# A hybrid decoder step on one core: weight splitting, softmax scaling and small copies are moved between VectorE, GpSimd and ScalarE, and a small inverse is spread over more steps

## The chip, the cores and the metric

The kernel runs on one core of a Trainium2 chip. The metric is device microseconds of the whole program, the median of several runs. TensorE multiplies matrices, VectorE (DVE in the profile), ScalarE (ACT) and GpSimd (POOL) work on elements, SyncE (SP) issues most transfers. Each engine executes its own instructions in order and waits on semaphores for the others.

## The reference

One layer of a decoder with a half-step SwiGLU FFN at either end and two groups of heads side by side in the middle. 256 prompt tokens and 8 decode tokens go through the same weights, 264 columns in all. The model width is 2048, the FFN width 5504, everything is float32.

```python
x = x + 0.5 * swiglu(rmsnorm(x, n1), f1g, f1u, f1d)
h = rmsnorm(x, nm)
proj = h @ w_in                                   # 38 tiles of 128 columns
o_att, k_buf, v_buf = attend(q, k, v, sinks)      # 16 query heads, 4 key/value heads, window 128
o_rwkv, shift, S = rwkv_time_mix(proj[..., ATT_COLS:], shift0, wkv0, ...)   # 16 heads of 64
x = x + concatenate([o_att, o_rwkv], -1) @ w_out
x = x + 0.5 * swiglu(rmsnorm(x, n2), f2g, f2u, f2d)
y = rmsnorm(x, final_norm)
```

Attention adds a relative bias, takes the maximum with a learned sink, and divides by the sum of the exponentials and the sink's own. In the RWKV part

```python
a = sigmoid(a0 + al @ a2); kk = k * k_k; k = k * (1 + (a - 1) * k_a)
S = S * exp(logw) + (S @ -kk) outer (kk * a) + v outer k;  y = S @ r      # for each token
```

## The kernel before, in words

**Layout.** Activations are kept transposed: a tile has 128 features on the partitions and the 264 tokens as columns. A weight tile of 128x128 is the stationary operand, an activation tile the moving one.

**Weights.** `chunk` loads up to four weight tiles (128x512 float32) with a transfer on SP's queue into a `raw` buffer (six of them). ScalarE rounds it to a `hi` part (line 123). A `tensor_tensor` subtraction on the engine that `chunk` is given computes the remainder `lo` (line 58 is the helper for all such operations); before the change it is VectorE in every case. There are four `hi` and four `lo` buffers. `gemm` then multiplies each weight tile three times (hi by hi, hi by lo, lo by hi) into an `acc` bank. A chunk's operations are emitted at high priority.

**Stages.** First FFN, then the mixing stage, then the second FFN. In the mixing stage `win` multiplies the 38 projection tiles one after the other: two for the low-rank parts, 24 for the eight pairs of RWKV heads (receptance, key, value), four for keys and values (`LKV` = 26 is the first of them), eight for queries. Then three passes of the output projection each take some of the 16 `mixed` tiles and add to all 16 output tiles:

```python
PASS = [[0,1,2,3],[8,9,10,11,4,5],[6,7,12,13,14,15]]      # 0-7 RWKV pairs, 8-15 attention tiles
```

Pass 0 thus has one chunk of four weight tiles for each output tile; passes 1 and 2 have a chunk of four and one of two.

**Tasks.** All the small work of the mixing stage is written as generators that are stepped once (`tick`) after every chunk of `win` and of the output projection; this sets the order of the program. `prep` prepares a pair of RWKV heads; `chain` does a batch of two pairs (four batches); `attend` does two prompt heads; `kvtask` writes keys and values; `dec_load` and `dec_attend` do the decode tokens' attention for four query tiles at once. The scheduler then orders the instructions of each engine by priority and by a model of when they become ready, so that the steps of a task are laid between chunks, not exactly where they were written.

**The chain of a batch.** When both `prep` are done, `X` and `Y` (tag `Xt`) are read back from DRAM, rearranged so that a 32x32 triangular block lies in the columns of one partition. After `DWAIT` steps, 30 elimination steps of two VectorE operations each run, with a step of the task after each `NSTEP` of them. `Y` is stored to DRAM (`scr2`, `sb` in the profile) by four transfers and read back by four as `TT`, now with rows on partitions. After `DWAIT` more steps VectorE adds the unit diagonal to the four blocks of `TT` and transposes two of them into `TN`. TensorE completes the 64x64 inverse from it. A product gives `W` and the values; VectorE copies the value part into `uv` in four pieces (line 595). State and output follow, three more chunk states are scanned, and `gnorm` normalises (reciprocals at line 677). `X`, `Y` and `TN` have one buffer each, `uv` three, of which the decode caches take two at a time.

**Softmax.** For each head VectorE adds the bias and takes the maximum, ScalarE exponentiates, VectorE forms the reciprocal of the sum and scales both parts (128x256 and 128x128; line 65 is the helper). TensorE transposes the result.

**Decode attention** waits in `dec_load` for a batch to be done (the third for the first call, the last for the second), loads its caches into `uv` buffers, and clears `qb`, which shares two `bk` buffers with `prep` and with the scores of `dec_attend`.

Of the kernel before, what the change touches and what calls it, by code (L numbers as in the profile page):

```python
# [9 lines left out]
AF = mybir.ActivationFunctionType  # L10
ALU = mybir.AluOpType
AX = mybir.AxisListType

P = 128
# [7 lines left out]
NPAIR = 8  # L22
NSH = 26
NIN = 38
HALF = (slice(0, 64), slice(64, 128))
# [4 lines left out]
NS, NO, NY, NH, NT, NLD = 38, 8, 8, 40, 18, 6  # L30
NWARM = 14
NGM, NKR, NUV, NTT, NBT = 10, 5, 3, 2, 5
NSTEP = 4
DWAIT = (8,8,8,4)
PW = (2, 1, 3, 2, 2)
ALPHA = math.exp(-0.5)
LKV = 26
# [5 lines left out]
VMU, VKK, VKA, VA0, VRK, VLW, VLB, VSK, VSD = 64, 90, 98, 106, 114, 122, 130, 138, 154  # L43
# [4 lines left out]
def body(tc, I, O):  # L48
    nc = tc.nc
    V, A, G, TE, SP = nc.vector, nc.scalar, nc.gpsimd, nc.tensor, nc.sync  # L50
    cnt = [0]

    def uid(s):
        cnt[0] += 1
        return f"{s}{cnt[0]}"

    def tt(e, out, a, b, op):
        return e.tensor_tensor(out=out, in0=a, in1=b, op=op)  # L58
# [4 lines left out]
    def ts(e, out, a, s1, op0, s2=None, op1=None):  # L63
        k = {} if op1 is None else dict(op1=op1)
        e.tensor_scalar(out=out, in0=a, scalar1=s1, scalar2=s2, op0=op0, **k)

    def act(out, in_, f, **k):
        return A.activation(out=out, in_=in_, func=f, **k)  # L68

    def bc(ap, shape):  # L70
        return ap.broadcast_to(list(shape))
# [23 lines left out]
    with ExitStack() as ctx:  # L95
# [20 lines left out]
        def chunk(src, n, e, ahead=True):  # L116
            w = n * P
            with tc.high_priority() if ahead else nullcontext():
                raw = wp.tile([P, CH * P], F32, tag="raw", bufs=NRAW, name=uid("raw"))
                hi = wp.tile([P, CH * P], F32R, tag="hi", bufs=NHL, name=uid("hi"))  # L120
                lo = wp.tile([P, CH * P], F32R, tag="lo", bufs=NHL, name=uid("lo"))
                SP.dma_start(raw[:, :w], src)  # L122
                A.copy(hi[:, :w], raw[:, :w])  # L123
                tt(e, lo[:, :w], raw[:, :w], hi[:, :w].bitcast(F32), ALU.subtract)
            return hi, lo

        def gemm(ps, src, xs, step=None, rng=None, ahead=True):
            n = len(xs)
            for k0 in range(0, n, CH):
                k1 = min(n, k0 + CH)  # L130
                if rng and k0 not in rng:
                    continue
                hi, lo = chunk(src[:, k0 * P:k1 * P], k1 - k0, V, ahead)
                for k in range(k0, k1):
                    xh, xl = xs[k]
                    c = slice((k - k0) * P, (k - k0 + 1) * P)
                    mm(ps[:, :T], hi[:, c], xh, k == 0, False)
                    mm(ps[:, :T], hi[:, c], xl, False, False)
                    mm(ps[:, :T], lo[:, c], xh, False, k == n - 1)
                if step:  # L140
                    step()

        vec = cp.tile([P, NVEC], F32, name="vec")
# [13 lines left out]
        def vc(i):  # L157
            return vec[:, i:i + 1]
# [173 lines left out]
        def mixing_body(mx, n2, n3, XD):  # L332
            def fix(shape, name):
                return mx.tile(list(shape), F32, name=name)
# [9 lines left out]
            ident, bo, cm = C[:, CID:CID + P], C[:, CBO:CBO + P], C[:, CCM:CCM + P]  # L344
# [8 lines left out]
                G.memset(pj[:, 0:1], 0.0)  # L353
            nmu = fix((P, NSH), "nmu")
            mu = vec[:, VMU:VMU + NSH]
            ts(V, nmu, mu, -1.0, ALU.mult, 1.0, ALU.add)
            tt(V, ss, ss, bc(mu.unsqueeze(2), (P, NSH, NB)), ALU.mult)
            nbat = len(BATCH)
# [2 lines left out]
            mixed = [None] * 16  # L361
            have = [False]

            def win(t):
                ps = acc()
                gemm(ps, I["win"][t], n2.xs, tick)
                if not have[0]:
                    n2.rstd(rs)
                    have[0] = True
                return ps  # L370
# [20 lines left out]
            def prep(p, bt, k, xrr, xk, xv):  # L391
# [7 lines left out]
                sg, a = tmp(), tmp()  # L399
# [20 lines left out]
                rk = tmp((P, T + 2 * NB))  # L420
                stt(b, b, 1e24, kk, ALU.min, ALU.mult)
                tt(V, b, b, a, ALU.mult)
                ts(V, a, a, 1.0, ALU.subtract, vc(VKA + p), ALU.mult)
                kx = a
                stt(kx, a, 1.0, xk, ALU.add, ALU.mult)
                stt(rk[:, :T], xrr, vc(VRK + p), kx, ALU.mult, ALU.mult)
# [43 lines left out]
                for h in range(2):  # L470
# [3 lines left out]
                    for blk in range(2):  # L474
                        x = blk * 32
# [12 lines left out]
                for c in range(4):  # L488
                    for h in range(2):
                        r, o = HALF[h], HALF[1 - h]  # L490
# [24 lines left out]
            def chain(bt):  # L515
                n = bt.n
                while bt.left:
                    yield
                nr = n * 16
                ng = P // nr  # L520
                if ng == 3:
                    ng = 2
                nj = 32 // ng
                X = ring((ng * nr, 32, 32), "X", 1)
                Y = ring((ng * nr, nj, 32), "Xt", 1)
# [4 lines left out]
                TT = ring((P, n * 4, 64), "TT", NTT)  # L530
                for h in range(2):
                    G.memset(TT[h * 64 + 32:h * 64 + 64, :, 0:32], 0.0)
                yield from pause(DWAIT[bt.i])
                for s in range(1, 31):
                    m, w = -(-s // ng), 31 - s
                    t = ring((ng * nr, m, w), "st", 2)
                    shp = (ng * nr, m, w)
                    tt(V, t, bc(X[:, s:s + 1, s + 1:], shp), bc(Y[:, :m, s:s + 1], shp), ALU.mult)
                    tt(V, Y[:, :m, s + 1:], Y[:, :m, s + 1:], t, ALU.add)
                    if s % NSTEP == 0:  # L540
                        yield
                for g in range(ng):
                    SP.dma_start(scr2[bt.i].rearrange("r (j g t) -> g r j t", g=ng, t=32)[g], Y[g * nr:(g + 1) * nr])
                yield from pause(1)
                for h in range(2):
                    for blk in range(2):
                        x = h * 64 + blk * 32
                        SP.dma_start(TT[x:x + 32, :, blk * 32:blk * 32 + 32],
                                     scr2[bt.i].rearrange("(h b m) (s t) -> h b s m t", h=2, b=2, s=32)[h, blk])
                yield from pause(DWAIT[bt.i])  # L550
                for h in range(2):
                    for blk in range(2):
                        x = h * 64 + blk * 32
                        v = TT[x:x + 32, :, blk * 32:blk * 32 + 32]
                        tt(V, v, v, bc(ident[x:x + 32, x:x + 32].unsqueeze(1), (32, n * 4, 32)), ALU.add)
                TN = ring((P, n * 4, 32), "TN", 1)
                for h in range(2):
                    V.transpose(TN[h * 64:h * 64 + 32], TT[h * 64:h * 64 + 32, :, 0:32])
# [1 line left out]
                ps = mp()  # L560
                for k in range(n):
                    for c in range(4):
                        for h in range(2):
                            j = k * 4 + c
# [7 lines left out]
                ps = mp()  # L572
# [9 lines left out]
                uv = bt.UV  # L582
# [8 lines left out]
                for k in range(n):  # L591
                    v = wus[k].rearrange("p (c t) -> p c t", c=4)
                    A.copy(W[:, k], v[:, 1:4, 0:64])
                    for h in range(2):
                        V.tensor_copy(uv[HALF[h], :, k, HALF[h]], v[HALF[h], :, 64:128])  # L595
                yield
                pbs = [mp() for _ in range(n)]
                for k in range(n):
                    for c in range(1, 4):
                        x = (c - 1) * P  # L600
# [6 lines left out]
                for k in range(n):  # L607
                    v = pbs[k][:, :384].rearrange("p (c t) -> p c t", c=3)
# [3 lines left out]
                for k in range(n):  # L612
                    for c in range(4):
                        x = (k * 4 + c) * 64
# [3 lines left out]
                for k in range(n):  # L618
                    for c in range(4):
                        x = (k * 4 + c) * 64  # L620
# [8 lines left out]
                for c in range(1, 4):  # L629
                    ps = mp()  # L630
# [4 lines left out]
                    for k in range(n):  # L635
                        for h in range(2):
                            r = HALF[h]
                            x = (k * 4 + c) * 64
# [20 lines left out]
                for k in range(n):  # L659
                    p, o = bt.p0 + k, Ys[k]  # L660
# [42 lines left out]
            def softmax(s, mxv, sinks, n):  # L703
                nm, sm, es = (ring((P, 2), "st" + x, 6) for x in "abc")
                ts(V, nm[:, :n], mxv[:, :n], -1.0, ALU.mult)
                for j in range(n):
                    act(s[j], s[j], AF.Exp, bias=nm[:, j:j + 1], accum_out=sm[:, j:j + 1])
                act(es[:, :n], nm[:, :n], AF.Exp, bias=sinks)
                tt(V, sm[:, :n], sm[:, :n], es[:, :n], ALU.add)
                V.reciprocal(sm[:, :n], sm[:, :n])  # L710
                for j in range(n):
                    ts(V, s[j], s[j], sm[:, j:j + 1], ALU.mult)

            def attend(t, q):
                p = t // 4
# [114 lines left out]
            for kind, i in SEQ:  # L830
                if kind == "b":
                    bt = newbatch(i)
                    for k in range(BATCH[i]):
                        p = bt.p0 + k
                        x = [shifted(2 + 3 * p + j, tmp()) for j in range(3)]
# [5 lines left out]
                elif kind == "kv":  # L841
                    w, p = i // 2, i % 2
                    ps = win(LKV + i)
                    x = slot()
# [4 lines left out]
                else:  # L849
                    ps = win(LKV + 4 + i)  # L850
# [5 lines left out]
                    if i % 4 == 3:  # L856
                        p = i // 4
                        d = spawn(dec_attend(p, qs[4 * p:]))
# [18 lines left out]
            k0 = 0  # L877
            for pi, ks in enumerate(PASS):
                now = need(ks)
                drain(now, [g for g in tasks if g not in now])  # L880
                with tc.high_priority():
                    for k in ks:
                        split(k)
                for o in range(KD):
                    ps = acc()
                    gemm(ps, I["wout"][o, :, k0 * P:(k0 + len(ks)) * P], [mixed[k] for k in ks], tick)
                    with tc.high_priority():
                        tt(V, xr[o], ps[:, :T], xr[o], ALU.add)
                    if pi == len(PASS) - 1 and o < CH:
                        n3.split(xr[o], tag="y")  # L890
                for k in ks:
                    mixed[k] = None
                k0 += len(ks)
# [42 lines left out]
        n2, n3 = Norm(VGM), Norm(VG2)  # L936
# [105 lines left out]
```

## Time and profile before

| | |
|---|---|
| median of 3 runs | 2026.01 us (2024.55 to 2027.55) |
| profiled execution, its own time | 2027.84 us |
| its span, first to last instruction | 2026.1 us |
| granted TensorE clock, mean | 0.994 |
| first FFN, about | 0 to 770 us |
| mixing stage, about | 770 to 1260 us |
| second FFN, about | 1260 to 2026 us |

A row of a group gives line, engine, operation, tiles and shapes, the count, then busy time in us and the mean ns of one, then the engine's idle time just before these instructions and what ended most of it. A row of the timeline gives start, duration, engine, line, operation and in brackets the idle time before and its releaser. A row of stretches gives busy time and count for each engine, the granted TensorE clock (PEclk, 1.00 is full), the share of time that the DMA engines were busy, and GB/s. In the chain of waits a row gives start, length and what the time went to.

### The profile page before, as it was taken

To read this page: it belongs to the slowest core of one execution; us is meant where nothing else is said; L and a number is where in the kernel's file an instruction comes from. 1 tells how busy PE (TensorE), PEld (TensorE's weight loads), DVE (VectorE), ACT (ScalarE), POOL (GpSimd) and SP (SyncE) were. 2 spreads that over 40 slices of the span, in tenths; PEclk is the share of its full clock that TensorE was granted. 3 is DMA by queue.
4 is the path that set the end of the run, shared out by engine and by line. 5 is a ranking of instruction groups with operands and counts; after the bars stand their busy time and mean duration, and the time that the engine had idled before them with its cause. 6 is when DMAs were issued, how large, how long until landed. Compare 5 with 4: busy or idle time off the path is not lost.

```text
span 2026.1 us, 45592 instructions
## 1 busy us (share of the span) xinstructions
PE 1994.1 (98%) x17126; PEld 1956.0 (97%) x17126; DVE 1324.4 (65%) x2674; ACT 1041.4 (51%) x2054; POOL 240.8 (12%) x342
## 2 busy tenths in 40 slices
PE   9999999999999999999999899999999999999998
PEld 9999999999999999998888789999999999999998
DVE  5865555655556577678778766775666666566665
ACT  5644444444444466665454555554444444444445
POOL 0401001010110122111110000120101101010012
PEclk9999999999999999999999999999999999999999
DMA  6565565655556566554456335565565555655654
GB/s 228 177 187 196 183 192 189 186 184 177 185 171 191 181 205 205 154 157 124 141 148 174 117 102 188 172 185 176 191 182 194 180 191 190 187 191 180 197 180 144
DMA packets 228798, 358.73 MB, mean 177 GB/s; under 512 B 42568, under 2 KB 83680, under 8 KB 228576
## 3 DMA queue, kind: packets, MB, share of 16 engines
q1 hardware_dynamic: 222112, 347.28, 54.6%
q10 hardware_dynamic: 6464, 8.54, 1.3%
q8 instruction: 134, 2.20, 0.4%
q14 instruction: 88, 0.72, 0.1%
HBM read 347.58 MB, written 10.22 MB: 177 GB/s over the span
## 4 chain that ended last, share of the span: by engine, by line
PE 94%; DVE 2%; DMA 2%; ACT 1%; SPq 1%; issue 1%; ACTq 0%; DVEq 0%
PE acc L74 85%; PE m L74 8%; DVE lo L58 1%; DMA TT<-sb 0%; DMA sb<-Xt 0%; DVE y L58 0%; DMA raw<-in_gu 0%; DMA ld<-in_sT 0%; DVE st L58 0%; SPq L122 0%; DVE Xt L58 0%; ACT t L68 0%; DVE uv L595 0%; DMA Xt<-sa 0%; PE m L495 0%
## 5 line engine op out<-in xcount | busy, mean ns | idle before, releaser
L58 DVE TENSOR_TENSOR lo<-raw,hi 128x512 fp32r<-128x512 f32 (+2 forms) x1304 | 871.8, 673 | 552.5 <-ACT hi L123 526.5
L123 ACT CAST hi<-raw 128x512 fp32r<-128x512 f32 (+2 forms) x1304 | 779.3, 602 | 861.6 <-PE acc L74 776.3
L74 PE MATMUL acc<-s,hi 128*128 128x264 f32 x5940 | 1107.3, 286 | 3.9 <-DVE s L58 1.6
L74 PEld LDWEIGHTS acc<-s,hi 128*128 128x128 f32 x5940 | 922.9, 188 | 10.0 <-ACT hi L123 2.2
L74 PE MATMUL acc<-s,lo 128*128 128x264 f32 x2970 | 848.3, 286 | 4.4 <-DVE lo L58 4.4
L74 PEld LDWEIGHTS acc<-s,lo 128*128 128x128 f32 x2970 | 559.5, 189 | 9.1 <-DVE lo L58 5.6
L74 PE MATMUL acc<-t,hi 128*128 128x264 f32 x2752 | 503.1, 284 | 0.0
L74 PEld LDWEIGHTS acc<-t,hi 128*128 128x128 f32 x2752 | 426.4, 188 | 0.0
L74 PE MATMUL acc<-t,lo 128*128 128x264 f32 x1376 | 389.0, 285 | 0.0
L58 POOL TENSOR_TENSOR t<-t,t 128x264 f32<-128x264 f32 (+1 forms) x148 | 150.7, 1018 | 1150.6 <-ACT hi L123 790.4
L74 PEld LDWEIGHTS acc<-t,lo 128*128 128x128 f32 x1376 | 258.4, 188 | 0.1
L74 PE MATMUL acc<-y,hi 128*128 128x264 f32 x648 | 124.5, 284 | 0.0
L74 PEld LDWEIGHTS acc<-y,hi 128*128 128x128 f32 x648 | 101.3, 188 | 0.2
L74 PE MATMUL acc<-y,lo 128*128 128x264 f32 x324 | 92.2, 285 | 0.0
L58 DVE TENSOR_TENSOR t<-acc,t 128x264 f32<-128x264 f32 x156 | 67.4, 432 | 36.8 <-PE acc L74 36.5
L58 POOL TENSOR_TENSOR o<-o,o 128x264 f32<-128x264 f32 x43 | 36.4, 846 | 222.7 <-ACT o L68 217.8
L74 PE MATMUL acc<-o,hi 128*128 128x264 f32 x324 | 62.8, 284 | 0.0
L74 PEld LDWEIGHTS acc<-y,lo 128*128 128x128 f32 x324 | 60.7, 187 | 0.0
L61 DVE SCALAR_TENSOR_TENSOR s<-acc,s 128x264 f32<-128x264 f32 x96 | 40.5, 427 | 16.0 <-PE acc L74 15.5
L74 PEld LDWEIGHTS acc<-o,hi 128*128 128x128 f32 x324 | 50.0, 188 | 0.0
L74 PE MATMUL m<-s,hi 128*128 128x264 f32 x260 | 48.5, 285 | 0.0
L61 DVE SCALAR_TENSOR_TENSOR x<-acc,x 128x264 f32<-128x264 f32 x96 | 40.5, 426 | 10.1 <-PE acc L74 9.6
(234 smaller groups left out, 1295.9 us busy)
## 6 DMA issues: line engine op xcount, KB each, us to landing
raw<-in_gu SPq DMA_DIRECT2D x688, 256.0 KB, 3.3
raw<-in_dn SPq DMA_DIRECT2D x224, 256.0 KB, 2.7
raw<-in_win SPq DMA_DIRECT2D x152, 256.0 KB, 3.5
raw<-in_dn SPq DMA_DIRECT2D x160, 192.0 KB, 2.7
raw<-in_wout SPq DMA_DIRECT2D x48, 256.0 KB, 3.3
raw<-in_wout SPq DMA_DIRECT2D x32, 128.0 KB, 2.9
xsp<-x ACTq DMA_DIRECT2D x16, 132.0 KB, 3.2
s<-xsp SPq DMA_DIRECT2D x16, 132.0 KB, 4.0
```

What stands on the lines that cost most here:

```text
L58: return e.tensor_tensor(out=out, in0=a, in1=b, op=op)
L61: return V.scalar_tensor_tensor(out=out, in0=a, scalar=s, in1=b, op0=op0, op1=op1)
L74: TE.matmul(out, lhsT, rhs, start=start, stop=stop, **k)
L123: A.copy(hi[:, :w], raw[:, :w])
```

## The change

- `gemm` counts the chunks of the whole program. Where `share` is set (query tiles of `win`, and all output-projection passes), chunks with an odd count have their `lo` computed by GpSimd, the others by VectorE.
- `NSTEP` goes from 4 to 2 and `DWAIT` from (8, 8, 8, 4) to (8, 8, 8, 8).
- The unit diagonal is no longer added to `TT` by VectorE: GpSimd writes ones on the diagonal of `Y` before it is stored, four memsets per batch.
- Of the four value copies of a batch, two go to ScalarE.
- Of the two softmax scalings of a head, the first goes to GpSimd, the second to ScalarE.
- In `prep`, `(a - 1) * k_a` goes from VectorE to ScalarE, as an activation with scale `k_a` and bias `-k_a`; `-k_a` is computed once on GpSimd.

```diff
-NSTEP = 4
-DWAIT = (8,8,8,4)
+NSTEP = 2
+DWAIT = (8, 8, 8, 8)
...
-        def gemm(ps, src, xs, step=None, rng=None, ahead=True):
+        nch = [0]
+
+        def gemm(ps, src, xs, step=None, rng=None, ahead=True, share=False):
...
-                hi, lo = chunk(src[:, k0 * P:k1 * P], k1 - k0, V, ahead)
+                nch[0] += 1
+                hi, lo = chunk(src[:, k0 * P:k1 * P], k1 - k0, G if share and nch[0] % 2 else V, ahead)
...
+            nka = fix((P, NPAIR), "nka")
+            ts(G, nka, vec[:, VKA:VKA + NPAIR], -1.0, ALU.mult)
...
-                gemm(ps, I["win"][t], n2.xs, tick)
+                gemm(ps, I["win"][t], n2.xs, tick, share=t >= LKV + 4)
...
-                ts(V, a, a, 1.0, ALU.subtract, vc(VKA + p), ALU.mult)
+                act(a, a, AF.Identity, scale=vc(VKA + p), bias=nka[:, p:p + 1])
...
+                for g in range(ng):
+                    d = Y[g * nr:(g + 1) * nr].rearrange("p j t -> p (j t)")
+                    G.memset(d[:, g:nj * 32:32 + ng], 1.0)
                 for g in range(ng):
                     SP.dma_start(scr2[bt.i].rearrange("r (j g t) -> g r j t", g=ng, t=32)[g], Y[g * nr:(g + 1) * nr])
...
-                for h in range(2):
-                    for blk in range(2):
-                        x = h * 64 + blk * 32
-                        v = TT[x:x + 32, :, blk * 32:blk * 32 + 32]
-                        tt(V, v, v, bc(ident[x:x + 32, x:x + 32].unsqueeze(1), (32, n * 4, 32)), ALU.add)
...
-                    for h in range(2):
-                        V.tensor_copy(uv[HALF[h], :, k, HALF[h]], v[HALF[h], :, 64:128])
+                    V.tensor_copy(uv[HALF[0], :, k, HALF[0]], v[HALF[0], :, 64:128])
+                    A.copy(uv[HALF[1], :, k, HALF[1]], v[HALF[1], :, 64:128])
...
-                for j in range(n):
-                    ts(V, s[j], s[j], sm[:, j:j + 1], ALU.mult)
+                ts(G, s[0], s[0], sm[:, 0:1], ALU.mult)
+                A.mul(s[1], s[1], sm[:, 1:2])
...
-                    gemm(ps, I["wout"][o, :, k0 * P:(k0 + len(ks)) * P], [mixed[k] for k in ks], tick)
+                    gemm(ps, I["wout"][o, :, k0 * P:(k0 + len(ks)) * P], [mixed[k] for k in ks], tick, share=True)
```

## The prediction

> **What bounds the kernel now.** I read the page first, then stretches of 5 us through the mixing stage (projections, RWKV chain, attention, output projection), the timelines of all engines where TensorE loses time, and the groups by form for prices.
>
> ```profile
> span 2026.1 us, 45592 instructions
> PE 1994.1 (98%) x17126; PEld 1956.0 (97%) x17126; DVE 1324.4 (65%) x2674; ACT 1041.4 (51%) x2054; POOL 240.8 (12%) x342
> 69.34 700.37 PE acc L74 x5760
> ```
>
> TensorE bounds it. The third row is a piece of the chain of waits in the first FFN: 700.37 / 5760 = 0.1216 us for a large matmul, so a full weight chunk (12 of them) is 1.46 us. The FFNs leave nothing to take and the change doesn't touch them. What can move lies in the mixing stage:
>
> ```profile
> core 0: us, PE busy (x) PEld busy (x) DVE busy (x) ACT busy (x) POOL busy (x), PEclk, DMA share, GB/s
> 915.00:920.00 5.00, 3.08 (x74) 3.01 (x76) 4.74 (x13) 0.38 (x2) 0.00 (x0) 0.84 0.33 91
> 965.00:970.00 5.00, 3.04 (x23) 2.62 (x22) 4.78 (x11) 1.17 (x2) 0.19 (x1) 1.00 0.32 74
> 995.00:1000.00 5.00, 3.92 (x89) 3.66 (x86) 4.81 (x14) 2.39 (x6) 0.39 (x2) 0.70 0.38 108
> 1045.00:1050.00 5.00, 2.92 (x22) 2.50 (x22) 4.75 (x11) 1.49 (x3) 1.90 (x6) 1.00 0.43 118
> 1100.00:1105.00 5.00, 3.12 (x19) 2.33 (x17) 5.00 (x20) 3.29 (x10) 1.44 (x2) 1.00 0.93 295
> 1145.00:1150.00 5.00, 4.00 (x56) 3.18 (x56) 3.71 (x18) 3.19 (x12) 0.00 (x0) 1.00 0.61 203
> 1150.00:1155.00 5.00, 2.61 (x26) 1.73 (x27) 3.14 (x9) 4.21 (x13) 0.00 (x0) 1.00 0.06 20
> 1155.00:1160.00 5.00, 3.56 (x11) 2.68 (x12) 4.98 (x15) 0.00 (x0) 1.63 (x7) 0.74 0.08 21
> 1160.00:1165.00 5.00, 3.38 (x15) 1.89 (x14) 2.01 (x10) 3.46 (x10) 1.06 (x7) 0.50 0.44 129
> 1165.00:1170.00 5.00, 4.89 (x20) 3.86 (x21) 3.44 (x11) 4.02 (x15) 2.46 (x4) 0.50 0.00 0
> 1170.00:1175.00 5.00, 5.00 (x34) 4.45 (x35) 4.03 (x19) 2.66 (x9) 0.49 (x1) 0.90 0.03 11
> sum 395.00, PE 375.10 PEld 340.96 DVE 301.84 ACT 221.14 POOL 40.31; mean PE 4.75 PEld 4.32 DVE 3.82 ACT 2.80 POOL 0.51
> ```
>
> The sum row covers 835 to 1230 us: TensorE idles 395.0 - 375.1 = 19.9 us there. That, with the clock that falls after idle stretches, is about all that any change here can win. The largest piece is 1145 to 1175, between the first and second output-projection pass: idle 1.00 + 2.39 + 1.44 + 1.62 + 0.11 = 6.56 us; the clock deficits times the busy time, 0.26 x 3.56 + 0.5 x 3.38 + 0.5 x 4.89 + 0.1 x 5.00, add 5.6. I call these 12.1 us the seam. In the five other stretches shown VectorE is at 4.7 us or more of 5 while TensorE starves: a late VectorE, after a stall of its own or under a backlog.
>
> ```profile
> 898.52 0.41 DVE L58 TENSOR_TENSOR TT<-TT,C 32x256 f32<-32x256 f32 x1 [4.29 <-DMA TT<-sb]
> 915.46 0.85 DVE L595 COPY uv<-m 64x256 f32<-64x256 f32 x2
> 916.83 0.86 DVE L595 COPY uv<-m 64x256 f32<-64x256 f32 x2
> 916.46 0.33 PE L74 MATMUL m<-BT,W 64*64 64x64 f32 x4 [1.89 <-DVE uv L595]
> 1152.21 0.33 PE L805 MATMUL m<-C,bk 128*128 128x128 f32 x1 [3.21 <-DVE bk L65]
> 1153.54 3.46 DVE L677 RECIPROCAL t<-t 128x264 f32<-128x264 f32 x2 [1.19 <-ACT t L68]
> 1161.45 0.37 ACT L744 COPY t<-m 128x256 f32<-128x256 f32 x1 [6.93 <-PE m L742]
> 1165.08 1.42 PE L74 MATMUL acc<-s,hi 128*128 128x264 f32 x3 [1.24 <-ACT s L870]
> ```
>
> First row: VectorE stands 4.29 us at the head of its queue for the readback of the inverse. Next three: TensorE waits until the value copies are done. Last four, the seam: the second pass needs the first decode attention; its softmax scaling (L65 on `bk`) ends late, then group norm of the last RWKV batch (L677) holds VectorE for 3.46 us in the middle, and large matmuls resume at 1165.08.
>
> **The change part by part.** Prices:
>
> ```profile
> L58 DVE TENSOR_TENSOR lo<-raw,hi 128x512 fp32r<-128x512 f32 x1112 | 771.7, 696 | 534.1 <-ACT hi L123 508.2 <-PE acc L74 10.7
> L58 DVE TENSOR_TENSOR TT<-TT,C 32x256 f32<-32x256 f32 x16 | 6.7, 417 | 12.8 <-DMA TT<-sb 12.5
> L595 DVE COPY uv<-m 64x256 f32<-64x256 f32 x16 | 6.7, 421 | 0.3
> L65 DVE TENSOR_SCALAR t<-t,stb 128x256 f32<-128x256 f32 x16 | 6.1, 381 | 0.3
> L65 DVE TENSOR_SCALAR t<-t,stb 128x128 f32<-128x128 f32 x16 | 4.5, 279 | 0.0
> L65 DVE TENSOR_SCALAR t<-t,vec 128x264 f32<-128x264 f32 x8 | 2.8, 350 | 0.0
> L500 ACT COPY BT<-m 64x256 f32<-64x256 f32 x16 | 5.9, 366 | 0.2
> L68 ACT ACTIVATE t<-t,sta 128x128 f32<-128x128 f32 x16 | 6.2, 388 | 0.0
> L58 POOL TENSOR_TENSOR t<-t,t 128x264 f32<-128x264 f32 x74 | 82.5, 1115 | 1105.7 <-ACT hi L123 790.4 <-DVE t L58 293.5 <-ACT t L68 21.8
> L58 POOL TENSOR_TENSOR s<-y,s 128x264 fp32r<-128x264 f32 x4 | 2.9, 744 | 41.3 <-PE m L74 40.0 <-ACT s L870 1.3
> L532 POOL MEMSET TT<- 32x256 f32 x8 | 2.4, 306 | 5.4 <-PE m L74 5.1
> ```
>
> *Chunks to GpSimd.* Counting chunks through the program, the first query chunk and the first chunk of each pass are odd. So GpSimd gets 16 of 32 query chunks, 8 of 16 in pass 0, and in passes 1 and 2 the four-tile chunk of every output tile (32), VectorE the two-tile ones: 56 x 0.696 = 39.0 us leave VectorE. No row shows a 512-wide one on GpSimd. From below: 0.744 us for 264 columns; without any fixed part 512 cost 1.44, with the memset's 0.31 as fixed part 1.15. From above: 1.115 x 512 / 264 = 2.16. I take 1.5, nearest to the undisturbed row with the same output type. TensorE needs 18 x 0.1216 = 2.19 us for an output tile of passes 1 and 2, so GpSimd keeps pace even at 2.16, barely, and four hi/lo pairs give some 5 us of cover. GpSimd and VectorE slow each other:
>
> ```profile
> 1320.93 0.84 DVE L58 TENSOR_TENSOR lo<-raw,hi 128x512 fp32r<-128x512 f32 x1 [0.64 <-ACT hi L123]
> 1326.50 0.69 DVE L58 TENSOR_TENSOR lo<-raw,hi 128x512 fp32r<-128x512 f32 x1 [0.43 <-ACT hi L123]
> ```
>
> The first ran beside a GpSimd operation in the second FFN, the second alone: 0.15 us each, at most 56 x 0.15 = 8 us of VectorE time back, well under 39.0. The Trainium skill (GPSIMD Engine Reference, Engine selection) speaks against this edit: elementwise work belongs on VectorE, two-input operations being about 2x slower on GpSimd. Doubling 0.696 would make an estimated 1.39 us, within the bounds above, still below 2.19; by the rule alone the sum would stay as it is. Whether the trace agrees at this width no row shows.
>
> *Softmax scaling.* 16 x 0.381 + 16 x 0.279 = 10.6 us leave VectorE; 16 on GpSimd at 0.4 to 1.1 us (VectorE's price; the 264-wide two-input row), 16 on ScalarE at 0.388. In a head's own chain this is 0 to 0.7 us longer, covered by other heads. The four decode scalings go the same way, two to each. Both engines now wait for the reciprocal with weight chunks queued behind: `hi` on ScalarE, `lo` on GpSimd, TensorE behind both.
>
> *Value copies.* Per batch two of four go to ScalarE (0.366): 0.84 us less between product and TensorE. Waits like the 1.89 us stand at two batches' tails (915 and 995): 1.7 us, and some clock: **-2**.
>
> *Unit diagonal.* 16 x 0.417 = 6.7 us leave VectorE, one add (0.42) per batch is on the way to TensorE. Added: four GpSimd memsets of the diagonal before the store, 0.1 to 0.31 each and a handover. SP's four stores wait for them, weight loads behind; six raw buffers, 8.8 us, cover that. The 4.29 us wait itself stays: the transpose now stands where the add stood. **0**, bounds -1.7 to +4.
>
> *Key scaling.* 8 x 0.350 leave VectorE; on ScalarE at most 0.388 x 264 / 128 = 0.80 each, with a handover there and back inside a preparation that has other work beside it: **0**, bounds -1 and +2.
>
> *NSTEP and DWAIT.* An inverse takes 15 task steps instead of 7, so all chain tails stand 8 steps later, the last 16 (its two waits go from 4 to 8). At one step per chunk that is 12 and 23 us or more. By the program's count the last chain still ends some 40 steps ahead of pass 2, its consumer. Its stores, readbacks and group norm now queue behind work of attention 0 to 3. The X/Y loads of the next batch, one buffer, fall at the step of this batch's readback; both wait on SP for the same store, weights behind: cover as above. **+1**, bounds -2 to +6.
>
> *The seam.* Ahead of it VectorE loses 24 of those chunks, 16.7 us, and half the prefill scalings, 5.3: 22 us, more than the 12.1 it lasts; group norm's 3.46 us falls later. Decode attention can start earlier, under pass 0. Bounds 0 and -12.1. I take **-7**: TensorE's and ScalarE's legs of it remain.
>
> The stretch at 1100 (VectorE 5.00 of 5, TensorE idle 1.88): **-1**. Late GpSimd halves: **+1.5** (one visible wait), bounds 0 and +20.
>
> Sum: -7 - 2 - 1 + 1 + 1.5 + 0 = -7.5 us. The profiled execution took 2027.84, 1.7 over its span; minus 7.5 gives 2020.3. Against the median of 2026.01, the middle of the runs, 2018.5: I say **2019**.
>
> **Rivals.**
>
> *One: the seam moves.* The first seam closes, but the last batch's chain and the second decode attention, which needs a value buffer of that batch, end after pass 1 has run dry. For it:
>
> ```profile
> 1158.11 0.31 POOL L771 MEMSET bk<- 128x256 f32 x1 [56.38 <-DVE t L61]
> 1215.02 0.56 POOL L823 COPY o<-bk 128x8 f32<-128x8 f32 x4 [44.53 <-ACT bk L821]
> ```
>
> The second decode attention delivers at 1215, just as pass 2 begins: no slack. Against it: 16 more chunks move off VectorE within pass 1. It gives back 5 to 9 of the 10 us won, so -7.5 becomes -2.5 to +1.5: 2023 to 2028. Chance 0.13: 0.09 "same", 0.02 on either side.
>
> *Two, slower: GpSimd stands.* It executes in order. The rows just shown had it waiting 56 and 45 us, free then because nobody needed it. If such a wait, or one of the 18 scalings, stands ahead of a weight half longer than the cover (5.8 us of chunks less 0.62 for `hi` and 1.5 for itself, some 3.7 us), TensorE stops. VectorE's like waits (965 and 1045) cost TensorE 1.96 and 2.08 us each. Six to ten such are 12 to 20 us, less the 9 of the other terms (-7 - 2 - 1 + 1): +3 to +11, and up to +18 where the seam stays too: 2029 to 2044. Against it: the order is laid out by expected readiness, and few GpSimd operations remain between halves. Chance 0.25.
>
> *Three, slower: GpSimd sets the pace.* If a half beside VectorE's own work takes 2.6 us, passes 1 and 2 grow by 32 x 0.41 = 13 us: about 2032. Only a wide form slower than proportional does it. Chance 0.08.
>
> *Four: all VectorE stalls go too*, about 20 us: 2006. Chance 0.06. That the edit isn't what it says I exclude.
>
> **How the numbers follow.** The forecast (2009 to 2021) has 0.48. A measurement tells about 0.2%, 4 us, from no change. Faster: 0.48 + 0.06 + 0.02 of rival one = 0.56; same 0.09; slower 0.25 + 0.08 + 0.02 = 0.35. Both signs hold much, so the forecast's own range stands beside the wide one: 2009 to 2021 against 2006 to 2036, which leaves out some 0.04 below (half of rival four and little else) and 0.13 above (half of rival two).
>
> **What would show it.** Right: VectorE busy near 1324 - 60 us; 56 `lo` on POOL at 1.3 to 1.9 us; no stretch of TensorE under 4 us of 5 between passes 0 and 1, clock 1.00 there; the readback wait of some 4 us now before the transpose. Wrong: TensorE waiting on `lo` of POOL or on a scaling, idle at the start of pass 2, more table loads on ScalarE than 30 (each 1.28 us by this row),
>
> ```profile
> L68 ACT ACT_TABLE_LOAD x30 | 38.5, 1283 | 4.4 <-PE m L74 2.7 <-PEq L1034 1.2
> ```
>
> or the seam as before.

## The result, and the profile after

| | before | after |
|---|---|---|
| median | 2025.57 us (2024.55 to 2027.55, 4 runs) | 2008.21 us (2007.07 to 2011.2, 4 runs) |
| profiled execution, its own time | 2027.84 us | 2008.12 us |
| mean granted TensorE clock | 0.994 | 0.998 |

The ratio is 0.9906, with a 95% interval of 0.9894 to 0.9918: faster by 0.94%, some 17 to 19 us. The forecast was 7.5 us. The sign and the place were right, the size was not: 2008.21 lies just outside the forecast's own range (2009 to 2021) and inside the wide one (2006 to 2036).

From the page of the changed kernel, its span and the busy time of each engine:

```profile
span 2006.0 us, 45669 instructions
PE 1980.9 (99%) x17126; PEld 1947.9 (97%) x17126; DVE 1300.9 (65%) x2550; ACT 1053.8 (53%) x2089; POOL 336.6 (17%) x433
```

The second FFN now begins about 19 us earlier. Stretches of the changed kernel: two at the start of pass 0, then the 30 us in which the seam lay before, then the sum's stretch of the prediction:

```profile
core 0: us, PE busy (x) PEld busy (x) DVE busy (x) ACT busy (x) POOL busy (x), PEclk, DMA share, GB/s
1110.00:1115.00 5.00, 4.37 (x47) 3.33 (x45) 2.96 (x11) 2.40 (x7) 2.24 (x6) 1.00 0.89 251
1115.00:1120.00 5.00, 4.47 (x34) 3.83 (x34) 2.66 (x13) 4.82 (x20) 4.57 (x13) 1.00 1.02 343
1145.00:1175.00 30.00, 30.00 (x275) 26.91 (x274) 20.91 (x58) 18.96 (x51) 12.20 (x12) 1.00 0.32 91
835.00:1230.00 395.00, 381.92 (x4007) 352.45 (x4006) 291.63 (x822) 242.46 (x608) 134.85 (x197) 1.00 0.53 149
```

Where the passes lie now is seen from the first transpose of the first decode attention, which pass 1 needs, and from the first two-tile half, which belongs to the first output tile of pass 1:

```profile
1111.07 0.27 PE L808 MATMUL m<-C,bk 128*128 128x128 f32 x1
1157.63 0.43 DVE L58 TENSOR_TENSOR lo<-raw,hi 128x256 fp32r<-128x256 f32 x1 [0.49 <-ACT hi L123]
```

Before, that transpose came at 1152.21 us, between the two passes. Now the first decode attention is done ahead of pass 0 (VectorE adds the first output tile of pass 0 at 1123 us), and pass 1 follows pass 0 at about 1160 us without a gap. Nothing of the seam's 12.1 us is left. The start of pass 0 idles 0.63 + 0.53 = 1.2 us, at full clock.

Over 835 to 1230 us TensorE idles 395.00 - 381.92 = 13.1 us, 19.9 before. Outside the seam that is 13.1 against 13.3: there the idle time has moved, not shrunk. To follow both losses I cut 770 to 1260 us of every kernel into 5 us stretches and added up the idle time (5 less TensorE's busy time) and the clock's deficit (one less PEclk, times the busy time): before 19.9 + 8.4 = 28.3 us, after 13.1 + 0.0. That is 15.2 of the 19.7 us between the two profiled executions, 12.1 of it the seam; the rest I can't place. (The sum is a guide only: over the kernels below it differs from the change of time by up to 6.5 us.)

In these two executions 8.4 of the 15.2 us are clock. That part varies from one execution to the next: of two variants below, `p_order` idles 22.6 us and lost 1.1 to the clock, `s_uv` 21.1 and 13.3. Over all executions the mean granted clock is 0.994 to 0.995 for the kernel before and 0.998 for the changed one, an estimated 6 to 7 us of 2008.

Where TensorE still waits, from the changed kernel's waits between 835 and 1230 us (engine and line, what it waited for: us in total, times, longest):

```profile
PE m L74 <- ACT t L68: 4.0, 4, 1.6
PE acc L74 <- DVE lo L58: 2.8, 3, 1.4
PE m L448 <- DVE S L61: 1.8, 1, 1.8
PE m L74 <- DVE st L58: 1.5, 2, 1.2
PE m L74 <- ACT uv L598: 1.3, 1, 1.3
```

No matmul waits for a weight half or a scaling of GpSimd (weight loads do once, for 0.2 us); before, `bk` of VectorE alone held it 3.21 us. The moved work, from the groups by form of the changed kernel:

```profile
L58 POOL TENSOR_TENSOR lo<-raw,hi 128x512 fp32r<-128x512 f32 x56 | 73.2, 1309 | 69.5 <-ACT hi L123 45.8 <-PE acc L74 17.3 <-DMA s<-xsp 2.5
L65 POOL TENSOR_SCALAR t<-t,stb 128x256 f32<-128x256 f32 x16 | 15.8, 988 | 18.6 <-DVE stb L713 8.0 <-ACT o L756 3.3 <-DVE st L58 3.2
L549 POOL MEMSET Xt<- 32x8 f32 x16 | 1.7, 105 | 33.1 <-DMA Xt<-sa 21.1 <-DVE st L58 10.9 <-PE acc L74 0.4
L715 ACT ACTIVATE t<-t,stb 128x128 f32<-128x128 f32 x16 | 6.4, 401 | 1.3 <-DVE stb L713 1.3
L68 ACT ACTIVATE t<-t,nka,vec 128x264 f32<-128x264 f32 x8 | 4.9, 608 | 12.0 <-DVE t L58 11.9
L68 ACT ACT_TABLE_LOAD x31 | 39.8, 1283 | 10.4 <-DVE S L61 4.9 <-PE m L74 2.1 <-DVE s L58 1.8
```

Every GpSimd duration lies inside its bounds; on ScalarE the softmax scaling took 0.401 us for the 0.388 taken, the key scaling 0.608, under its bound of 0.80, and there is one table load more. GpSimd does stand at the head of its queue (33.1 us ahead of the diagonal, 18.6 ahead of the scalings), and nobody pays for it in this order.

### The profile page after: what moved, and what is told of

The parts are those of the page before. It is cut to its first block, busy times and chain, and to the rows that moved or that the text cites. A ratio compares the mean times of both kernels' runs of the same rounds, so it can differ in the third digit from the quotient of the medians.

```text
span 2006.0 us, 45669 instructions
## 1 busy us (share of the span) xinstructions
PE 1980.9 (99%) x17126; PEld 1947.9 (97%) x17126; DVE 1300.9 (65%) x2550; ACT 1053.8 (53%) x2089; POOL 336.6 (17%) x433
## 4 chain that ended last, share of the span: by engine, by line
PE 92%; DVE 3%; DMA 2%; ACT 1%; issue 1%; SPq 1%; POOL 0%; DVEq 0%; ACTq 0%; POOLq 0%
PE acc L74 85%; PE m L74 7%; DVE lo L58 1%; DMA sb<-Xt 0%; DVE Xt L58 0%; DVE st L58 0%; DMA TT<-sb 0%; DMA raw<-in_win 0%; DMA raw<-in_gu 0%; ACT L68 0%; ACT hi L123 0%; DVE y L58 0%; SPq L122 0%; ACT t L68 0%; DMA Xt<-sa 0%
## 5 line engine op out<-in xcount | busy, mean ns | idle before, releaser
L58 DVE TENSOR_TENSOR lo<-raw,hi 128x512 fp32r<-128x512 f32 (+1 forms) x1248 | 853.4, 688 | 542.6 <-ACT hi L123 522.5
L58 POOL TENSOR_TENSOR lo<-raw,hi 128x512 fp32r<-128x512 f32 x56 | 73.2, 1309 | 69.5 <-ACT hi L123 45.8
```

## Experiments

Two theories stood at the start. *Relief*: what counts is VectorE time taken off ahead of the seam, so the shared chunks carry most of the gain. *Order*: any of the edits lays the stages out anew, and the gain is that of the order. Undoing one part at a time tells them apart: by relief the chunks must cost the most, by order no part has a price of its own.

**One part undone in the changed kernel.** `u_share` gives all chunks back to VectorE, `u_steps` the old step constants, `u_soft` both softmax scalings to VectorE, `u_small` the value copies, the unit diagonal and the key scaling together.

```diff
 u_share
-                hi, lo = chunk(src[:, k0 * P:k1 * P], k1 - k0, G if share and nch[0] % 2 else V, ahead)
+                hi, lo = chunk(src[:, k0 * P:k1 * P], k1 - k0, V, ahead)
 u_steps
-NSTEP = 2
-DWAIT = (8, 8, 8, 8)
+NSTEP = 4
+DWAIT = (8,8,8,4)
 u_soft
-                ts(G, s[0], s[0], sm[:, 0:1], ALU.mult)
-                A.mul(s[1], s[1], sm[:, 1:2])
+                for j in range(n):
+                    ts(V, s[j], s[j], sm[:, j:j + 1], ALU.mult)
 u_small
-                act(a, a, AF.Identity, scale=vc(VKA + p), bias=nka[:, p:p + 1])
+                ts(V, a, a, 1.0, ALU.subtract, vc(VKA + p), ALU.mult)
 ...
```

> The changed kernel with all weight halves back on VectorE (steps, scaling, diagonal, value copies and key scaling stay changed). Theory A (relief: the 17 us come from VectorE's load ahead of the seam, whose largest part are the 24 chunks, 16.7 us): the seam between passes 0 and 1 comes back in most of its length, 2018 to 2024 us. Theory B (order: they come from the chain tails being emitted 8 to 16 steps later, so that the first decode attention is ready before the last batch's group norm): still 2008 to 2012 us, no seam.

> The changed kernel with NSTEP = 4 and DWAIT = (8, 8, 8, 4) again. Theory A (relief): within 4 us of the changed kernel, 2006 to 2012 us, no seam. Theory B (order): the last batch's tail stands in front of the first decode attention again, the seam is back with a granted clock under 0.9 in it, 2018 to 2026 us.

> The changed kernel with both softmax scalings on VectorE again. Theory A (relief): 10.6 us of VectorE back, half of it ahead of the seam: 2010 to 2015 us. Theory B (order): within 3 us of the changed kernel, 2006 to 2011 us.

> The changed kernel with all four value copies, the unit diagonal and the key scaling on VectorE again. Theory A (relief, with the value copies on TensorE's path at the batches' tails): 2 to 4 us of idle TensorE back at the tails and some granted clock, 2010 to 2014 us. Theory B (order): within 2 us of the changed kernel, 2006 to 2010 us.

| kernel | median us | ratio to before (95%) | lost of the 0.94% |
|---|---|---|---|
| `u_share` | 2014.5 | 0.9936 (0.9921 to 0.9951) | 0.30 |
| `u_steps` | 2012.2 | 0.9930 (0.9915 to 0.9945) | 0.24 |
| `u_soft` | 2011.49 | 0.9928 (0.9911 to 0.9944) | 0.22 |
| `u_small` | 2015.64 | 0.9945 (0.9930 to 0.9960) | 0.39 |

Each loss is known to about 0.19 (the two intervals together). By these figures every part carries 4 to 8 us. Relief by the number of microseconds moved falls: 39.0 us of chunks are worth 0.30%, and some 13 us of small work (copies, adds, key scaling) 0.39%.

**One part alone on the kernel before.** If the parts add up, each alone brings what its undoing cost (additive); if the seam closes only when all are there, each alone brings little (joint).

```diff
 a_share: only the GpSimd chunks;  a_steps: only NSTEP and DWAIT;  a_soft: only the scalings
 a_small: only the value copies, the diagonal and the key scaling (the lines of the change)
```

> The kernel before with only the odd weight halves on GpSimd. Theory C (additive: each part is worth what its removal cost, 6 to 7 us here): 2019 to 2021 us. Theory D (joint: the seam closes only when several parts together take off more than it lasts, so parts alone win little and their sum stays under the 17 us): 2022 to 2027 us, seam shorter but there.

> The kernel before with only NSTEP = 2 and DWAIT = (8, 8, 8, 8). Theory C (additive, 5 us): 2020 to 2023 us. Theory D (joint): 2024 to 2028 us; group norm of the last batch moves out of the seam, but decode attention still starts late, since VectorE's load is as it was.

> The kernel before with only the two softmax scalings moved. Theory C (additive, 4 us): 2021 to 2024 us. Theory D (joint): 2024 to 2028 us.

> The kernel before with only half the value copies, the unit diagonal and the key scaling moved. Theory C (additive, 8 us): 2017 to 2020 us, idle of TensorE at the batches' tails (around 915, 995 and 1080 us) gone, seam as before. Theory D (joint): 2021 to 2025 us; the tails improve by 2 to 4 us and the rest of the 8 is not seen.

| kernel | median us | ratio to before (95%) | gain, % |
|---|---|---|---|
| `a_share` | 2023.56 | 0.9986 (0.9977 to 0.9996) | 0.14 |
| `a_steps` | 2022.47 | 0.9978 (0.9969 to 0.9988) | 0.22 |
| `a_soft` | 2023.29 | 0.9981 (0.9971 to 0.9990) | 0.19 |
| `a_small` | 2016.23 | 0.9946 (0.9931 to 0.9961) | 0.54 |

The four add up to 1.09%, against 0.94% for all: additive within the error of about 0.23. That each part keeps its price with and without the others, within the errors, speaks against order alone. But relief doesn't explain the prices either. From the page of `a_share`:

```profile
PE 1986.3 (98%) x17126; PEld 1952.3 (97%) x17126; DVE 1326.8 (66%) x2618; ACT 1041.1 (52%) x2054; POOL 312.7 (15%) x398
```

With 56 halves gone to GpSimd, VectorE is as busy as before (1324.4 us): the 39.0 us that were moved are not off it (the last section shows why). In the changed kernel the sharing takes 4.8 us off it (1305.7 in `u_share`, 1300.9). How the sharing comes to its 0.14 to 0.30% is open. And `a_steps`, which moves no work and leaves VectorE at 1324.1 us, is faster by the order alone: the first decode attention comes at 1120 us in place of 1152, ahead of the last batch's tail and not behind it. The kernels with the new steps (`a_steps`, the changed one, `u_share`, `u_soft`, `u_small`) have it at 1109 to 1125 us, those with the old ones (the kernel before, `a_share`, `a_soft`, `a_small`, `u_steps`) at 1137 to 1152.

No part alone closes the whole gap. From 1080 us on TensorE idles 10.0 us before, 6.4 to 8.8 with one part alone, 2.0 to 4.2 with one part undone, 1.7 with all. `a_soft` still waits between passes 0 and 1; in the other three that place is nearly closed, and a wait stands at the start of pass 0 instead. The longest waits of TensorE there, one row from each of `a_share`, `a_soft` and `a_steps`, from their waits:

```profile
PE m L743 <- DVE t L65: 8.1, 2, 7.7
```

```profile
PE m L805 <- POOL bk L65: 2.7, 1, 2.7
```

```profile
PE m L805 <- DVE bk L65: 4.2, 1, 4.2
```

With the chunks moved but the scaling left on VectorE, TensorE still waits for the scaling, 7.7 us at one go; with the scaling on GpSimd alone it waits there. Idle and clock loss are 26.0, 26.4 and 24.5 us (28.3 before): these three win from 1080 us on and lose a little ahead of it.

**The small moves split.** `s_uv` makes only the value copies' move, `s_diag` only the diagonal's.

```diff
 s_uv
-                    for h in range(2):
-                        V.tensor_copy(uv[HALF[h], :, k, HALF[h]], v[HALF[h], :, 64:128])
+                    V.tensor_copy(uv[HALF[0], :, k, HALF[0]], v[HALF[0], :, 64:128])
+                    A.copy(uv[HALF[1], :, k, HALF[1]], v[HALF[1], :, 64:128])
 s_diag
 ...
+                    G.memset(d[:, g:nj * 32:32 + ng], 1.0)
 ...
-                        tt(V, v, v, bc(ident[x:x + 32, x:x + 32].unsqueeze(1), (32, n * 4, 32)), ALU.add)
```

> The kernel before with only half the value copies moved to ScalarE. The three small moves together won 11 us. Theory E (value copies: TensorE's queue stands behind them at the batches' tails, and the clock falls after it): most of the 11, 2017 to 2021 us, the idle at 915, 995 and 1080 us gone. Theory F (unit diagonal: its adds stand at the head of VectorE's queue behind the readback): 2023 to 2027 us here.

> The kernel before with only the unit diagonal set on GpSimd before the store. Theory F (unit diagonal): 2017 to 2021 us, VectorE's wait for the readback shorter by its adds and less idle of TensorE at 965 and 1045 us. Theory E (value copies): 2024 to 2028 us; the transpose waits where the add waited.

`s_uv`: 2023.71 us, ratio 0.9993 (0.9983 to 1.0004), nothing that can be told from no change. `s_diag`: 2017.66 us, ratio 0.9961 (0.9951 to 0.9971), about 8 us, the largest gain of any single edit. Its 0.39, the copies' 0.07 and `a_small`'s 0.54 leave 0.08 +- 0.2 for the key scaling and what the three do to each other; it was not run alone.

A part of what the diagonal did is seen in VectorE's own queue. The timeline of the kernel before, VectorE and then TensorE, behind the readback of the second batch:

```profile
965.00 0.41 DVE L58 TENSOR_TENSOR TT<-TT,C 32x256 f32<-32x256 f32 x1 [3.29 <-DMA TT<-sb]
965.34 0.41 DVE L61 SCALAR_TENSOR_TENSOR t<-t,t 128x264 f32<-128x264 f32 x1
965.69 0.67 DVE L58 TENSOR_TENSOR lo<-raw,hi 128x512 fp32r<-128x512 f32 x1
966.39 0.86 DVE L58 TENSOR_TENSOR TT<-TT,C 32x256 f32<-32x256 f32 x2
967.28 0.43 DVE L558 STREAM_TRANSPOSE TN<-TT 32x256 f32<-32x256 f32 x1
967.75 0.42 DVE L58 TENSOR_TENSOR TT<-TT,C 32x256 f32<-32x256 f32 x1
968.20 0.69 DVE L58 TENSOR_TENSOR lo<-raw,hi 128x512 fp32r<-128x512 f32 x1
...
966.41 0.39 PE L74 MATMUL acc<-s,lo 128*128 128x264 f32 x1 [0.91 <-DVE lo L58]
968.95 0.39 PE L74 MATMUL acc<-s,lo 128*128 128x264 f32 x1 [1.05 <-DVE lo L58]
```

The stall of 3.29 us uses up the buffered weights, and then four adds, 1.7 us, stand between the halves that TensorE is out of: it waits 0.91 and 1.05 us for them. The same stands at 1044 to 1050. In `s_diag` the stall for the readback remains (11.5 us in 7 waits, 12.5 in 7 before), but the adds behind it are gone. The two places come 2 and 6 us earlier there. Its stretches around them and over the 30 us of the old seam, and the start of pass 0 in its timeline:

```profile
960.00:965.00 5.00, 4.74 (x39) 4.53 (x38) 2.37 (x6) 2.80 (x6) 0.00 (x0) 1.00 0.52 119
965.00:970.00 5.00, 5.00 (x43) 5.00 (x42) 5.00 (x11) 3.26 (x9) 1.87 (x3) 1.00 0.60 184
1040.00:1045.00 5.00, 3.69 (x31) 3.48 (x30) 4.60 (x10) 1.74 (x3) 2.22 (x6) 1.00 0.35 91
1045.00:1050.00 5.00, 5.00 (x68) 4.61 (x68) 4.20 (x10) 1.72 (x5) 2.01 (x4) 1.00 0.77 230
1145.00:1175.00 30.00, 28.15 (x207) 23.11 (x206) 25.30 (x79) 19.41 (x55) 6.40 (x17) 1.00 0.37 106
```

```profile
1100.93 0.43 DVE L556 STREAM_TRANSPOSE TN<-TT 32x256 f32<-32x256 f32 x1 [0.72 <-DMA TT<-sb]
...
1103.26 0.43 DVE L556 STREAM_TRANSPOSE TN<-TT 32x256 f32<-32x256 f32 x1 [1.46 <-DMA TT<-sb]
...
1104.33 0.55 DVE L65 TENSOR_SCALAR t<-t,stb 128x256 f32<-128x256 f32 x2
...
1104.93 0.48 PE L738 MATMUL m<-C,t 128*128 128x128 f32 x1 [6.62 <-DVE t L65]
```

At the two places TensorE idles 0.26 + 1.31 = 1.6 us, 1.96 + 2.08 = 4.0 before: 2.5 us won. But ahead of 1080 us its idle time is 10.0 us in all, as before (9.9), because other waits have grown. From 1080 us on it idles 8.4 in place of 10.0 us: 1.85 in place of 6.56 over the old seam, and a new wait of 6.62 us at the start of pass 0. The rest of the fall from 28.3 to 18.5 + 1.9 = 20.4 us is clock, 6.5 us, and that may belong to these two executions alone: over the ten of `s_diag` and the 30 of the kernel before that ran beside it the mean granted clock is the same, 0.9945. So the price of the adds, about 8 us, is measured; of its way to TensorE the 2.5 us behind the two stalls are seen, and the rest stays open.

The last four rows show what is left: the softmax scaling stands on VectorE behind two transposes that wait for the last readback, and TensorE idles 6.62 us for it. In the whole change the scaling is not on VectorE, and the last two of these transposes stand at 1086 and 1089 us. Either seems to do: `u_soft`, with the scaling on VectorE and everything else changed, has no such wait either (its last transposes stand at 1087 and 1088 us). Its longest wait for a scaling:

```profile
PE m L808 <- DVE bk L65: 1.6, 1, 1.6
```

**A new order alone.** In `prep` two VectorE operations that don't depend on each other change places, nothing else.

```diff
-                stt(KR[:, 0], c4(kk), -1.0, W[:, :, 0:64], ALU.mult, ALU.mult)
                 tt(V, KR[:, 1], c4(xrr), W[:, :, 1:65], ALU.mult)
+                stt(KR[:, 0], c4(kk), -1.0, W[:, :, 0:64], ALU.mult, ALU.mult)
```

> The kernel before with two independent VectorE operations of the preparation exchanged (the first two products into kr); the same work on the same engines in another order. If the parts' gains are what they remove: within 2 us of the kernel before, 2024 to 2028 us. If a new order alone is worth as much as a part: 3 us or more off, to either side.

2027.47 us, ratio 1.0005 (0.9996 to 1.0014): nothing that can be measured, though idle and clock loss (22.6 + 1.1 us) are spread otherwise than before. One such shuffle doesn't give 0.2%, let alone 0.94; it doesn't exclude that another would, and the new steps, which change the order and no work, do.

**More sharing.** From the changed kernel: GpSimd takes every other chunk from the first projection tile on.

```diff
-                gemm(ps, I["win"][t], n2.xs, tick, share=t >= LKV + 4)
+                gemm(ps, I["win"][t], n2.xs, tick, share=True)
```

> The changed kernel with odd weight halves on GpSimd for all 38 projection tiles, not from the queries on: 60 more leave VectorE where it is busy at 5.00 of 5 us in several stretches. Relief theory: 3 to 6 us faster than the changed kernel, 2002 to 2006 us. Rival two of the prediction (GpSimd stands: here its queue holds the copies of the preparation and the diagonal, which wait up to 10 us for ScalarE and for transfers, with halves behind them): TensorE waits for halves of POOL, 2010 us or slower.

2030.36 us, ratio 1.0021 (1.0010 to 1.0031): 22 us more than the changed kernel and slower than the one before. Idle and clock loss are 23.9 + 12.5 us, nearly all of the excess over the changed kernel ahead of 1080 us. One of its stretches, and the timeline there:

```profile
1010.00:1015.00 5.00, 1.35 (x28) 1.00 (x26) 4.50 (x20) 2.40 (x8) 1.51 (x4) 0.97 0.25 80
```

```profile
1010.47 0.43 DVE L58 TENSOR_TENSOR pj<-acc,rs 128x264 f32<-128x264 f32 x1
...
1010.93 0.51 ACT L68 ACTIVATE t<-pj,vec 128x256 f32<-128x256 f32 x1 [5.12 <-DVE pj L58]
1010.96 0.71 POOL L382 COPY shc<-pj 128x9 f32<-128x9 f32 x1 [7.38 <-DVE pj L58]
1012.09 0.32 ACT L596 COPY W<-m 128x192 f32<-128x192 f32 x1 [0.65 <-POOL shc L382]
1013.37 0.37 ACT L598 COPY uv<-m 64x256 f32<-64x256 f32 x1 [0.96 <-DVE uv L597]
1013.78 0.33 PE L74 MATMUL m<-BT,W 64*64 64x64 f32 x4 [3.35 <-ACT uv L598]
```

VectorE is in the elimination (pairs of 0.22 us operations) and comes to the projection tile `pj` late; ScalarE stands 5.12 us and GpSimd 7.38 us at the heads of their queues for it, and the value copies that TensorE needs are behind. So a longer in-order wait decides, as the slower rival had it, but here TensorE's wait ends with ScalarE's copy; for halves on GpSimd only its weight loads wait, 1.3 us in 5 times.

That VectorE is late fits with what GpSimd's halves do to it. Its page has VectorE busy for 1303.4 us, no less than the 1300.9 of the changed kernel, though 60 more halves (41.8 us at 0.696) have left it. One place where the time went:

```profile
998.55 1.26 POOL L58 TENSOR_TENSOR lo<-raw,hi 128x512 fp32r<-128x512 f32 x1
998.58 1.52 DVE L61 SCALAR_TENSOR_TENSOR t<-pj,nmu,t 128x264 f32<-128x264 f32 x1
```

In the kernel before such an operation takes 0.486 us on average; this one began under a GpSimd half and ended 0.29 us after it. I added up all VectorE operations between 770 and 1260 us that took over 0.1 us more than the median of their tile and shape in the kernel before, counting the excess. Ahead of 1080 us it is 34.5 us here and 6.1 in the changed kernel, and every one of these operations began under a GpSimd operation. That this excess makes TensorE's loss there was not isolated.

## Why the prediction was right, and where its sizes failed

*The direction.* TensorE lost time to a late VectorE at a few places, and the largest of them, the seam, went from 12.1 us to nothing, with the clock at 1.00. GpSimd kept the pace: 1.309 us a half against the 1.5 taken, never near 2.19. Rivals one to three did not happen in this kernel. Of the four, the fourth (all stalls go, 2006) came nearest in time, though 13.1 us of idle time stay.

*The seam, -7.* It gave 12.1, the whole bound. Its place was right and so was "decode attention can start earlier", but not the reason: 22 us of VectorE relief ahead of it, most of it from chunks. `a_share` shows that the chunks relieve VectorE of nothing, and in `u_share`, without them, TensorE is busy throughout 1145 to 1175 us all the same. What goes with the closed seam is the first decode attention ahead of pass 0, and that came with the new steps, which I had priced as a loss. That this term had the right sign is in part luck.

*The unit diagonal, 0 with bounds -1.7 to +4.* The step that failed most. It alone is worth about 8 us, outside its bounds. I priced the adds by what lies between readback and TensorE's first matmul of the inverse ("one add per batch is on the way"), and kept the stall as fixed. What I left out is who is queued behind them: right after a 3 to 4 us stall the weight halves are used up, so the adds delay the halves that TensorE is out of. The stretches at 965 and 1045 that I quoted had these waits in them; I put them down to the stall alone. They are 2.5 of the 8 us; where the rest comes from is open. In the changed kernel the waits for the readback stand before the transposes, as forecast, the longest 2.6 us.

*The steps, +1 with bounds -2 to +6.* Wrong in sign and outside the bounds: -4.5 us alone, 5 lost when undone. The count of steps held: in `a_steps` the product of the values (`m<-gm,uv`) comes 14, 12 and 23 us later in the first, second and last batch, 5 earlier in the third. What I put at nothing is what can go ahead of those tails: the first decode attention (1120 for 1152 us) and the inverses of the second and third batch (`TN` at 947.9 and 1025.0 us, 967.3 and 1047.0 before).

*The stretch at 1100, -1.* TensorE idled 1.88 us there and 0.61 at 1119 us before; the start of pass 0 now idles 1.2.

*The clock outside the seam* (8.4 - 5.6 = 2.8 us in the profile before, none after) I had left to "some clock".

*The value copies, -2.* Nothing measurable alone (0.07% +- 0.1, or 1.4 +- 2 us), so the term is neither shown nor excluded. TensorE waits for the copies of the other engine instead: `m<-BT,W` on `ACT uv` is in the waits after.

*The key scaling, 0*, and *late GpSimd halves, +1.5.* The first can't be told from 0; the second is about 0.

*VectorE's busy time* was to fall by some 60 us; it fell by 1324.4 - 1300.9 = 23.5. The term that was mis-sized is the slowing by GpSimd, 8 us at most in the working, taken from one pair of rows. The 32 two-tile halves alone took 32 x (1.007 - 0.418) = 18.8 us more, from the groups of the kernel before and the changed one:

```profile
L58 DVE TENSOR_TENSOR lo<-raw,hi 128x256 fp32r<-128x256 f32 x32 | 13.4, 418 | 0.2 <-ACT hi L123 0.2
```

```profile
L58 DVE TENSOR_TENSOR lo<-raw,hi 128x256 fp32r<-128x256 f32 x32 | 32.2, 1007 | 0.9 <-ACT hi L123 0.8
```

With all other delayed operations the excess, counted as above, is 30.4 us, against the 39.0 that the chunks were to bring. Most of it, 24.4 us, falls behind 1080 us, where it cost no time that can be seen: TensorE is busy throughout passes 1 and 2. In `x_allshare` more of it falls where VectorE is late.

*The wide range.* The chance of 0.25 for a slower kernel by sharing was not idle: extended to the 30 projection tiles ahead of the queries, it is slower than the kernel before, if by another way than a standing GpSimd.

## What to carry to other kernels

Right behind an in-order wait on a critical engine, what is buffered has just been used up, and small operations queued there delay what TensorE is out of: look at what stands behind each stall before moving large work whose time is hidden. After moving work from VectorE to GpSimd, read VectorE's busy time again: here 39.0 us of halves moved away took nothing off it, and the same sharing turned into a loss by where in the program it starts. Parts that each look small in their own row added up here, and the largest single gap closed by a change of order as much as by moved work.

## What the hardware showed that was not expected

*A two-input VectorE operation waits for the end of a two-input GpSimd one.* From the changed kernel's timeline in pass 2, one half on each engine, and VectorE's accumulation between them:

```profile
1205.70 1.30 POOL L58 TENSOR_TENSOR lo<-raw,hi 128x512 fp32r<-128x512 f32 x1 [0.91 <-ACT hi L123]
...
1205.82 0.43 DVE L58 TENSOR_TENSOR s<-acc,s 128x264 f32<-128x264 f32 x1 [0.34 <-PE acc L74]
1206.18 1.10 DVE L58 TENSOR_TENSOR lo<-raw,hi 128x256 fp32r<-128x256 f32 x1
```

GpSimd's half ends at 1205.70 + 1.30 = 1207.00; VectorE's ends at 1206.18 + 1.10 = 1207.28, and in all 27 pairs of passes 1 and 2 in which a two-tile half began under one of GpSimd it ends 0.28 or 0.29 us after GpSimd's, whether it began 0.25 or 0.67 us after it. It is not slowed by a factor, it waits. The accumulation, one input of which is a bank of PSUM (the memory that TensorE writes its sums to), took its usual 0.43 us under the same GpSimd operation. The Trainium skill (SBUF — State Buffer, SBUF: two separate sides) states this as a rule: the port pair that the two engines share is locked for a whole instruction by whichever comes first, and a VectorE operation takes part if it has two inputs in SBUF. The trace agrees for both operations; and where VectorE's half began first (1077.18 us), it was GpSimd's that took longer, 1.50 us.

Under the one-input softmax scaling on GpSimd VectorE's half does not wait, which this rule would not lead one to expect:

```profile
1094.80 0.92 POOL L65 TENSOR_SCALAR t<-t,stb 128x256 f32<-128x256 f32 x1
1095.21 0.68 DVE L58 TENSOR_TENSOR lo<-raw,hi 128x512 fp32r<-128x512 f32 x1
```

It took its usual time, and so did the three other halves of the changed kernel that began under such a scaling.

*GpSimd's price depends on the form.* A two-input half of 512 columns took 1.309 us against 0.696 on VectorE, 1.88 times; the one-input scaling of 256 columns by a value for each partition 0.988 against 0.381, 2.6 times (0.92 to 0.95 us in 12 of the 16, still 2.4 times). For the first, the Trainium skill (GPSIMD Engine Reference, Engine selection) gives about 2x, and the trace agrees; its "roughly line-rate" for one input is not what the second row shows.
